# Start places of the normed rows, rows of a norm by transposes, and the order of the last sums, in a two-layer hybrid trunk on one core

## The chip, the core and the metric

The kernel runs on one core of one Trainium2 chip. TensorE (PE in the profile; PEld is its weight load) multiplies, VectorE (DVE), ScalarE (ACT) and GpSimd (POOL) do the elementwise work, SyncE (SP) issues most DMAs. The metric is the device time of one execution in microseconds, lower is better. All arrays are float32; the large products are made from two roundings of each operand (below).

## What is computed

A trunk of two layers on 512 tokens of width 1024. Layer 0 mixes tokens with a gated delta rule, layer 1 with sliding-window attention on a key and value projected once from layer 0's result; each layer ends with a gated MLP with a short causal convolution.

```python
def rmsnorm(x, w):
    xf = x.astype(jnp.float32)
    y = xf * lax.rsqrt(jnp.mean(xf * xf, axis=-1, keepdims=True) + EPS)
    return (y * w.astype(jnp.float32)).astype(x.dtype)

def conv_gated_mlp(hn, w_up, conv_w, conv_b, w_down):
    u = causal_dwconv(hn @ w_up, conv_w, conv_b)
    gate, val = jnp.split(u, 2, axis=-1)
    return (jax.nn.silu(gate) * val) @ w_down

def reference(x, ...):
    h = x
    for layer in range(2):
        if layer == 0:
            h = h + gated_deltanet(rmsnorm(h, a_norm_w[0]), ...)
        else:
            k_sh, v_sh = shared_kv(h, kv_norm_w, w_kv)
            h = h + sliding_window_sink_attention(rmsnorm(h, b_norm_w[0]), k_sh, v_sh, ...)
        h = h + conv_gated_mlp(rmsnorm(h, ffn_norm_w[layer]), ...)
    return rmsnorm(h, final_norm_w)
```

## The kernel before

The residual `h` lies transposed: eight tiles of 128 features by 512 tokens. A norm is split: `normed` (L888) multiplies each tile by the norm's weight and splits it into a rounded part (`xh`, ScalarE, L175) and the remainder (`xl`, VectorE, L176); the factor of each token, 1/rms, is applied after the product. So a normed input is sixteen rows of 128 x 512, eight `xh` and eight `xl`. The helper `row(tag)` (L110) takes each from a ring of eight buffers, and every buffer is exactly 2048 bytes per partition.

A product with a normed input is `mm3` (L161): for each of the eight k, three matmuls with 512 columns,

```python
PE.matmul(ps, hi[:, k, :m], xh[k], start=first and k == 0, stop=False)
PE.matmul(ps, hi[:, k, :m], xl[k][:], start=False, stop=False)
done.append(PE.matmul(ps, lo[:, k, :m], xh[k], start=False, stop=last and k == kt - 1))
```

which are L165, L166 and L167 of the profile; `hi` and `lo` (`whi`, `wlo`) are the weights, split in the same way by `cast` (L131, lines L135 on ScalarE and L136 on VectorE). The stationary operand is the weight block, the moving one is the row of the normed input. `mm3` serves the projections of the delta rule (until about 460 us), the up-projections of both MLPs (about 520 to 820 us and 1040 to 1330 us) and the key and value projection; the queries of attention have the same three matmuls in `one_by_one` (L1307, L1309, L1311). The down-projections (L1051 to L1053) have 256 columns and rows from other tags.

The factor of a norm comes in two functions. `rstd_cols` (L856) sums squares over the eight tiles, turns the sum into one column per block of 128 tokens (four matmuls with one column, L867), and gives `rt`, 128 x 4, by a square root and a reciprocal. `rstd_rows` (L873) spreads `rt` over all partitions: VectorE makes four scaled identities (L876, 128 x 512), TensorE multiplies a block of ones with them (L883, plain float32, 512 columns, two instructions), and ScalarE copies the result to `rstd` (L885, tile `p6s`). It is called three times: in both MLPs and in attention.

`final` (L1200) is the last norm. All but the last of the eight tiles have their weighted copy (`hw`) and their squares ready before the last down-projection, which is cut into two halves of 256 tokens (`last_down`, L960 to L962, twice for each half). When a half is done, `finish(u)` (L1230) weighs and squares the last tile's 256 tokens, turns the back four tiles of each block (L1218), sums the squares into columns (L1239), makes the factor (L1240 on ScalarE, L1241 on VectorE) and scales the turned blocks, the back half row on ScalarE (L1246), the front half row on VectorE (L1248); each half row goes out by its own DMA of 256 KB on SP (L1249).

The framework's scheduler orders each engine's instructions by priority, within the order of the code; `tc.high_priority` moves an instruction up, and `together` (L185) keeps a group in one piece on its engine; `behind(later, earlier)` (L179) fixes that one comes after another on the same engine without a semaphore.

Of the kernel before, what the change touches and what calls it, by code (L numbers as in the profile page):

```python
# [11 lines left out]
AF = mybir.ActivationFunctionType  # L12
ALU = mybir.AluOpType
# [4 lines left out]
P = 128  # L18
T = 512
NC = T // P  # L20
D = 1024
KD = D // P
EPS = 1e-6
# [21 lines left out]
def kernel(  # L45
# [27 lines left out]
    V, S, G, PE, SP = nc.vector, nc.scalar, nc.gpsimd, nc.tensor, nc.sync  # L73
# [9 lines left out]
    def nm(s):  # L83
        cnt[0] += 1
        return f"{s}_{cnt[0]}"
# [4 lines left out]
    main = ctx.enter_context(tc.tile_pool(name="main", bufs=1))  # L90
    PAIRS = {"sy": 4, "nt": 2, "kT": 2, "qT": 2, "at": 2, "ktok": 2, "vt": 2, "pz": 2, "m32": 1}
    ROWS = {
        "xh": 8,
        "xl": 8,
        "acc": 2,
        "sz": 2,
        "va": 2,
        "dt": 4,
        "ol": 1,
        "zl": 1,  # L100
# [6 lines left out]
        "f": 3,  # L107
    }

    def row(tag, dt=F32, n=T):  # L110
        return main.tile([P, n], dt, tag=tag, bufs=ROWS[tag], name=nm(tag))

    def pair(tag, dt=F32):
# [2 lines left out]
    def bank(tag):  # L116
        return psum.tile([P, T], F32, tag=tag, bufs=BANKS[tag], name=nm(tag))

    def const(shape, dt=F32, s="c"):
        return cp.tile(list(shape), dt, name=nm(s))  # L120
# [19 lines left out]
    def load_rows(w, tags):  # L140
        rows = [row(t)[:].rearrange("p (k c) -> p k c", k=2) for t in tags]
        for i, r in enumerate(rows):
            SP.dma_start(r, tiles_of(w, 2 * i * P, 2, 0))
        return rows
# [34 lines left out]
    def behind(later, earlier):  # L179
        info = mybir.DependencyInfo(mybir.DependencyClass.NoSync, mybir.DependencyReason.DATA)  # L180
        tc.add_manual_dep(later.ins, earlier.ins.name, info, reason="order of issue")
# [3 lines left out]
    def together(makes, *after):  # L185
        first = None
        for make in makes:
            if first is None:
                first = make()
                for a in after:  # L190
                    behind(first, a)
            else:
                with tc.high_priority(JUMP):
                    behind(make(), first)
# [16 lines left out]
    for i in range(2):  # L211
        cs = slice(HQK * P + i * P, HQK * P + (i + 1) * P)
# [4 lines left out]
    ident = const([P, P], s="ident")  # L217
# [3 lines left out]
    ones = const([P, P], s="ones")  # L221
    V.memset(ones[:], 1.0)
    epsc = const([P, 1], s="eps")
    V.memset(epsc[:], EPS)
    onec = ones[:, 0:1]
# [4 lines left out]
    def columns(parts, n, s, q=SP, tag="acc", place="g"):  # L230
        st = row(tag, n=P)
        r = 0
        for ap in parts:
            k = ap.shape[0]
            q.dma_start(st[r : r + k, :], ap)
            r += k
        ps = bank(place)
        PE.transpose(ps[:, :n], st[:n, :], ident[:n, :n])
        t = const([P, n], s=s)
        V.tensor_copy(t[:], ps[:, :n])  # L240
        return t
# [11 lines left out]
        q=S,  # L253
# [125 lines left out]
    def hc(ap):  # L379
# [397 lines left out]
    for pos, word in enumerate(" ".join(ORDER).split(), 1):  # L777
        name, _, later = word.partition("@")
        a, n = name[0], [int(d) for d in name[1:]]
# [33 lines left out]
    def nxt(role, tags):  # L813
        turn[role] = turn.get(role, -1) + 1
        return tags[turn[role] % len(tags)]

    def r2(role, dt=F32):
        return row(nxt(role, ROLES[role]), dt)
# [4 lines left out]
    def third_stage():  # L823
        return main.tile([P, 6, 256], F32, tag="st3", bufs=1, name=nm("st3"))
# [25 lines left out]
    for m in range(KD):  # L850
        x3 = xrows[m].rearrange("p (c e) -> p c e", c=NC)
        SP.dma_start(x3, x[0, :, m * P : (m + 1) * P].rearrange("(c p) e -> p c e", p=P))
        pt = bank("g")
        turn_row(pt, xrows[m])
        S.copy(hT[m], pt[:])
    def rstd_cols(h):  # L856
        acc = None
        for k in range(KD):
            sq = r2("sum" if acc is None else "hsq")
            S.activation(sq[:], h[k], AF.Square)  # L860
            if acc is None:
                acc = sq
            else:
                V.tensor_tensor(acc[:], acc[:], sq[:], op=ALU.add)
        ps = bank("g")
        for c in range(NC):
            PE.matmul(ps[:, c : c + 1], acc[:, c * P : (c + 1) * P], onec, start=True, stop=True)  # L867
        rt = const([P, NC], s="rt")
        S.activation(rt[:], ps[:, 0:NC], AF.Sqrt, bias=epsc[:, 0:1], scale=1.0 / D)
        V.reciprocal(rt[:], rt[:])  # L870
        return rt

    def rstd_rows(h):  # L873
        rt = rstd_cols(h)
        dg = third_stage()[:, 0:2, :].rearrange("p k c -> p (k c)")
        V.tensor_tensor(  # L876
            dg[:].rearrange("p (c t) -> p c t", c=NC),
            ident[:].unsqueeze(1).to_broadcast([P, NC, P]),
            rt[:].unsqueeze(2).to_broadcast([P, NC, P]),
            op=ALU.mult,  # L880
        )
        ps = bank("g")
        PE.matmul(ps[:], ones[:], dg[:], start=True, stop=True)  # L883
        r = r2("rstd")
        S.copy(r[:], ps[:])  # L885
        return r
# [291 lines left out]
    for m2 in range(KD // 2):  # L1178
        srcs = [tiles_of(a_w_out[0], 1024 * u, 8, 256 * m2) for u in range(2)]
        sts = [load_stage(a_w_out[0], 1024 * u, 8, 256 * m2) for u in range(2)]  # L1180
        if m2 < 2:
            for j in range(2):
                m = 2 * m2 + j
                ps = bank("d")
# [15 lines left out]
    def final(h, last_down):  # L1200
        hw, acc = [], None
        for k in range(KD):
            t = r2("xh")
            hw.append(t)
            if k == KD - 1:
                break
            V.tensor_scalar(t[:], h[k], onw_c[:, 9 + k : 10 + k], None, op0=ALU.mult)
            sq = r2("sum" if acc is None else "hsq")
            S.activation(sq[:], h[k], AF.Square)
            if acc is None:  # L1210
                acc = sq
            else:
                V.tensor_tensor(acc[:], acc[:], sq[:], op=ALU.add)

        def turned(hf, c, tag):
            pt = bank(tag)
            for k in range(4):
                PE.transpose(pt[:, k * P : (k + 1) * P], hw[4 * hf + k][:, c * P : (c + 1) * P], ident[:])  # L1218
            return pt

        CUTS = [(0, 2), (2, 4)]
        parts = [bank("d") for _ in CUTS]
        S.activation(warm[:], acc[:, 0:1], AF.Sqrt)
        front = [turned(0, c, t) for c, t in enumerate(["s", "s", "p", "g"])]
        h7, w7 = h[KD - 1], hw[KD - 1]
        sq7 = r2("hsq")
        rt = const([P, NC], s="rt")
        ts = [slice(a * P, b * P) for a, b in CUTS]

        def finish(u):  # L1230
            c0, c1 = CUTS[u]
            cs = slice(c0, c1)
            V.tensor_scalar(w7[:, ts[u]], h7[:, ts[u]], onw_c[:, 16:17], None, op0=ALU.mult)
            S.activation(sq7[:, ts[u]], h7[:, ts[u]], AF.Square)
            back = [turned(1, c, "s" if u and c % 2 else "d") for c in range(c0, c1)]
            ps = bank("g")
            for c in range(c0, c1):
                for x in (acc, sq7):
                    PE.matmul(ps[:, c : c + 1], x[:, c * P : (c + 1) * P], onec, start=x is acc, stop=x is sq7)  # L1239
            S.activation(rt[:, cs], ps[:, cs], AF.Sqrt, bias=epsc[:, 0:1], scale=1.0 / D)  # L1240
            V.reciprocal(rt[:, cs], rt[:, cs])  # L1241
            for c in range(c0, c1):
                for hf, pt in enumerate((front[c], back[c - c0])):
                    y = r2("xl")
                    if hf:
                        S.activation(y[:], pt[:], AF.Copy, scale=rt[:, c : c + 1])  # L1246
                    else:
                        V.tensor_scalar(y[:], pt[:], rt[:, c : c + 1], None, op0=ALU.mult)  # L1248
                    SP.dma_start(out[0, c * P : (c + 1) * P, hf * T : (hf + 1) * T], y[:])  # L1249

        n = len(CUTS)
        for u in range(n):
            ps = parts[u][:, 0 : ts[u].stop - ts[u].start]
            last_down(ps, ts[u], 0)
            if u > 0:
                finish(u - 1)
            last_down(ps, ts[u], 1)
            V.tensor_tensor(h7[:, ts[u]], h7[:, ts[u]], ps, op=ALU.add)
        finish(n - 1)


    Vp = main.tile([P, NC, 256], F32, tag="m32", bufs=1, name="Vp")
# [281 lines left out]
```

## Time and profile before

| | |
|---|---|
| median of the runs | 1399.07 us (1398.06 to 1400.09, 2 runs) |
| the profiled execution | 1399.55 us |
| its span on the core | 1397.4 us |
| granted TensorE clock over the span | 0.998 |
| VectorE, ScalarE, GpSimd busy | 82%, 55%, 1% of the span |

A matmul's busy time in the profile is longer than the step from one matmul to the next, since matmuls are pipelined. So for a dense stretch the reader takes the starts of consecutive matmuls in the timeline and subtracts them. A weight load runs beside the matmul ahead of it.

### The profile page before, as it was taken

The numbers are of one execution on the slowest core, as the hardware profiler recorded it, in microseconds if no ns is written. First come the engines' busy times: TensorE is split into PE (matmuls) and PEld (weight loads), VectorE is DVE, ScalarE is ACT, GpSimd is POOL, SyncE is SP. The second block draws the span as 40 slices with busy tenths as digits, with TensorE's granted clock in tenths as the row PEclk, the third lists the DMA queues.
The fourth block names the chain that finished last, engine by engine and source line by source line (L and its number), as shares of the span: only waits on it lengthen the run. The fifth ranks groups of instructions, "written<-read, shape, count | busy, mean of one in ns | idle before, by whom it ended". The sixth has DMA issues, their size and how long they took to land.

```text
span 1397.4 us, 22194 instructions
## 1 busy us (share of the span) xinstructions
PE 1374.6 (98%) x8514; PEld 1171.0 (84%) x8514; DVE 1144.3 (82%) x2153; ACT 765.6 (55%) x1482; POOL 15.2 (1%) x33
## 2 busy tenths in 40 slices
PE   7999999999999999999999999999999999999998
PEld 5788887888887898888988889877788889988897
DVE  4896896978967998879968899788668889878996
ACT  7766465757557455444344445677545444444543
POOL 1000000000100000000000000000000000000000
PEclk9999999999999999999999999999999999999999
DMA  5234154162567334221343223312132221432222
GB/s 162 83 114 134 50 173 141 64 197 91 171 192 225 127 119 140 94 88 52 130 151 121 76 84 114 121 62 69 61 113 91 91 95 63 146 106 80 96 76 76
DMA packets 164029, 154.97 MB, mean 111 GB/s; under 512 B 24340, under 2 KB 150869, under 8 KB 163925
## 3 DMA queue, kind: packets, MB, share of 16 engines
q1 hardware_dynamic: 161666, 153.37, 34.3%
q8 instruction: 67, 1.10, 0.3%
q10 hardware_dynamic: 2259, 0.20, 0.1%
q14 instruction: 37, 0.30, 0.1%
HBM read 136.74 MB, written 15.75 MB: 109 GB/s over the span
## 4 chain that ended last, share of the span: by engine, by line
PE 90%; DVE 4%; ACT 3%; DMA 2%; issue 1%; SPq 0%; DVEq 0%; ACTq 0%
PE d L165 19%; PE d L167 19%; PE d L166 19%; PE g L201 2%; PE d L1053 2%; PE d L1051 2%; PE d L1052 2%; PE s L1053 1%; PE s L1051 1%; PE s L1052 1%; PE d L1307 1%; PE d L1311 1%; PE d L1309 1%; PE g L1053 1%; PE g L1052 1%; PE g L1051 1%
## 5 line engine op out<-in xcount | busy, mean ns | idle before, releaser
L166 PE MATMUL d<-xl,whi 128*128 128x512 f32 x1128 | 443.0, 395 | 0.0
L165 PE MATMUL d<-xh,whi 128*128 128x512 f32 x1128 | 442.6, 395 | 0.4 <-DVE va L1284 0.3
L167 PE MATMUL d<-xh,wlo 128*128 128x512 f32 x1128 | 442.5, 394 | 0.0
L135 ACT CAST whi<-stage 128x1024 fp32r<-128x1024 f32 (+2 forms) x238 | 231.6, 977 | 224.9 <-PE d L166 129.3
L136 DVE TENSOR_TENSOR wlo<-stage,whi 128x1024 fp32r<-128x1024 f32 (+2 forms) x238 | 268.1, 1129 | 51.8 <-ACT whi L135 50.5
L165 PEld LDWEIGHTS d<-xh,whi 128*128 128x128 f32 x1128 | 211.7, 188 | 44.8 <-DVE va L1284 0.7
L167 PEld LDWEIGHTS d<-xh,wlo 128*128 128x128 f32 x1128 | 211.7, 188 | 44.5 <-DVE wlo L136 0.7
L166 PEld LDWEIGHTS d<-xl,whi 128*128 128x128 f32 x1128 | 211.7, 188 | 43.4 <-issue 0.7
L283 DVE SCALAR_TENSOR_TENSOR acc<-d,cwc,acc 128x511 f32<-128x511 f32 (+2 forms) x96 | 70.2, 738 | 5.2 <-ACT acc L280 4.5
L933 ACT ACTIVATE dt<-dt 128x512 f32<-128x512 f32 x44 | 27.8, 632 | 80.2 <-DVE dt L916 80.2
L911 DVE TENSOR_TENSOR sz<-d,p6s 128x512 f32<-128x512 f32 x58 | 39.9, 688 | 37.6 <-PE d L167 35.3
L916 DVE SCALAR_TENSOR_TENSOR va<-sz,fcw,va 128x511 f32<-128x511 f32 (+1 forms) x58 | 43.4, 747 | 1.7 <-ACT va L914 0.9
L916 DVE SCALAR_TENSOR_TENSOR dt<-sz,fcw,dt 128x511 f32<-128x511 f32 (+1 forms) x58 | 43.3, 746 | 1.7 <-ACT dt L914 0.9
L564 DVE TENSOR_TENSOR sT<-sT,p6s 64x31 f32<-64x31 f32 (+15 forms) x124 | 40.8, 329 | 1.6
L1376 ACT ACTIVATE dt<-dt,sm 128x256 f32<-128x256 f32 (+1 forms) x64 | 30.1, 471 | 21.5 <-DVE sm L1359 21.5
L558 DVE TENSOR_TENSOR p6s<-sN,sT 64x31 f32<-64x31 f32 (+15 forms) x124 | 40.6, 327 | 1.5
L135 ACT CAST whi<-st 128x768 fp32r<-128x768 f32 (+1 forms) x30 | 23.8, 792 | 31.5 <-PE g L1052 8.6
L911 DVE TENSOR_TENSOR zl<-d,p6s 128x512 f32<-128x512 f32 x30 | 20.6, 688 | 23.0 <-PE d L167 22.7
L693 ACT ACTIVATE rq<-o 128x128 f32<-128x128 f32 x64 | 19.0, 297 | 35.7 <-DVE o L688 26.1
L935 DVE TENSOR_TENSOR va<-dt,va 128x512 f32<-128x512 f32 x44 | 30.4, 690 | 1.3
L136 DVE TENSOR_TENSOR wlo<-st,whi 128x768 fp32r<-128x768 f32 (+1 forms) x30 | 26.9, 900 | 2.1 <-ACT whi L135 1.7
L914 ACT ACTIVATE dt<-sz,normc,fcw 128x512 f32<-128x512 f32 x29 | 23.6, 815 | 7.3 <-DVE sz L911 7.1
(859 smaller groups left out, 2975.6 us busy)
## 6 DMA issues: line engine op xcount, KB each, us to landing
stage<-in_ffn_w_up_dram SPq DMA_DIRECT2D x44, 1024.0 KB, 5.0
stage<-in_a_w_in_dram SPq DMA_DIRECT2D x23, 1024.0 KB, 5.2
stage<-in_ffn_w_down_dram SPq DMA_DIRECT2D x16, 768.0 KB, 4.9
stage<-in_a_w_out_dram SPq DMA_DIRECT2D x8, 1024.0 KB, 6.0
st<-in_ffn_w_down_dram SPq DMA_DIRECT2D x8, 768.0 KB, 5.2
zd<-sz SPq DMA_DIRECT2D x16, 256.0 KB, 2.0
od<-o SPq DMA_DIRECT2D x16, 256.0 KB, 2.4
stage<-in_b_w_q_dram SPq DMA_DIRECT2D x4, 1024.0 KB
```

The lines of the kernel that those rows point to most:

```text
L135: S.copy(hi[:, :kt, :m], src)
L136: V.tensor_tensor(lo[:, :kt, :m], src, hi[:, :kt, :m].bitcast(F32), op=ALU.subtract)
L165: PE.matmul(ps, hi[:, k, :m], xh[k], start=first and k == 0, stop=False)
L166: PE.matmul(ps, hi[:, k, :m], xl[k][:], start=False, stop=False)
L167: done.append(PE.matmul(ps, lo[:, k, :m], xh[k], start=False, stop=last and k == kt - 1))
L283: V.scalar_tensor_tensor(acc[:, d:], ps[:, : T - d], col, acc[:, d:], op0=ALU.mult, op1=ALU.add)
L564: V.tensor_tensor(Tm[:, s + 1 : 32, 0:m], Tm[:, s + 1 : 32, 0:m], tv, op=ALU.subtract)
L911: V.tensor_tensor(u[:], ps[:], rs[:], op=ALU.mult)
L916: V.scalar_tensor_tensor(acc[:, d:], u[:, : T - d], tap(2 - d, t), acc[:, d:], op0=ALU.mult, op1=ALU.add)
L1051: PE.matmul(ps, w[0][:, wk, :], hi, start=first and k == 0, stop=False, **kw)
L1052: PE.matmul(ps, w[0][:, wk, :], lo, start=False, stop=False, **kw)
L1053: PE.matmul(ps, w[1][:, wk, :], hi, start=False, stop=k == n - 1, **kw)
```

## The change

It has three parts.

**Places.** A buffer of `xh` or `xl` gets 16 elements more (2112 bytes, 64 more than a multiple of 512), and the row is a view that begins 0 to 12 elements into it. In the built program of before, the sixteen rows begin at 0 modulo 512 bytes, and so do all other tiles of the pool and the weight tiles `whi` and `wlo`. After, the rows begin at

| row k | 0 | 1 | 2 | 3 | 4 | 5 | 6 | 7 |
|---|---|---|---|---|---|---|---|---|
| `xh`, bytes modulo 512 | 0 | 64 | 128 | 192 | 256 | 336 | 416 | 496 |
| `xl`, bytes modulo 512 | 8 | 80 | 160 | 240 | 288 | 320 | 384 | 448 |

and all other tiles of the pool still at 0 modulo 512. Of each pair, one begins at a multiple of 64 bytes and the other 8, 16, 32 or 48 bytes off one.

**Rows of the norm.** `rstd_rows` makes its rows by four transposes of a column of `rt` that is repeated 128 times, in place of the scaled identities and the product with ones.

**The end.** In `finish`, the sums of squares move ahead of the last tile's transposes; for the second half, the sum over seven tiles and that over the last one go to banks of their own and the first enters the square root as its bias, column by column; the front half row of block 1 moves from the first to the second half, behind the last tile's weighing; the last half row's DMA goes out on ScalarE's queue.

```diff
+    SHIFTS = {"xh": [0, 0, 0, 0, 0, 4, 8, 12], "xl": [2, 4, 8, 12, 8, 0, 0, 0]}
+    taken = {"xh": 0, "xl": 0}
+
     def row(tag, dt=F32, n=T):
+        if tag in SHIFTS:
+            t = main.tile([P, T + 16], dt, tag=tag, bufs=ROWS[tag], name=nm(tag))
+            d = SHIFTS[tag][taken[tag] % 8]
+            taken[tag] += 1
+            return t[:, d : d + n]
         return main.tile([P, n], dt, tag=tag, bufs=ROWS[tag], name=nm(tag))
...
     def rstd_rows(h):
         rt = rstd_cols(h)
-        dg = third_stage()[:, 0:2, :].rearrange("p k c -> p (k c)")
-        V.tensor_tensor(
-            dg[:].rearrange("p (c t) -> p c t", c=NC),
-            ident[:].unsqueeze(1).to_broadcast([P, NC, P]),
-            rt[:].unsqueeze(2).to_broadcast([P, NC, P]),
-            op=ALU.mult,
+        ps = bank("g")
+        together(
+            [
+                lambda c=c: PE.transpose(ps[:, c * P : (c + 1) * P], rt[:, c : c + 1].to_broadcast([P, P]), ident[:])
+                for c in range(NC)
+            ]
         )
-        ps = bank("g")
-        PE.matmul(ps[:], ones[:], dg[:], start=True, stop=True)
         r = r2("rstd")
         S.copy(r[:], ps[:])
         return r
...
-        def finish(u):
-            c0, c1 = CUTS[u]
-            cs = slice(c0, c1)
-            V.tensor_scalar(w7[:, ts[u]], h7[:, ts[u]], onw_c[:, 16:17], None, op0=ALU.mult)
+        def finish(u, left):
+            cs, at = range(*CUTS[u]), slice(*CUTS[u])
             S.activation(sq7[:, ts[u]], h7[:, ts[u]], AF.Square)
-            back = [turned(1, c, "s" if u and c % 2 else "d") for c in range(c0, c1)]
-            ps = bank("g")
-            for c in range(c0, c1):
-                for x in (acc, sq7):
-                    PE.matmul(ps[:, c : c + 1], x[:, c * P : (c + 1) * P], onec, start=x is acc, stop=x is sq7)
-            S.activation(rt[:, cs], ps[:, cs], AF.Sqrt, bias=epsc[:, 0:1], scale=1.0 / D)
-            V.reciprocal(rt[:, cs], rt[:, cs])
...
+            weighed = V.tensor_scalar(w7[:, ts[u]], h7[:, ts[u]], onw_c[:, 16:17], None, op0=ALU.mult)
+            if left:
+                behind(left(), weighed)
+            back = {c: bank("s" if u and c % 2 else "d") for c in cs}
+            for c in cs:
+                turn_into(back[c], 1, c, range(3))
+            ps = bank("d" if u else "g")
+            if u:
+                sums = bank("g")
+                columns_of(sums, acc, cs)
+                V.tensor_scalar(rest[:, at], sums[:, at], 1.0 / D, EPS, op0=ALU.mult, op1=ALU.add)
+                summed = columns_of(ps, sq7, cs)
...
+            for c in cs:
+                behind(turn_into(back[c], 1, c, [3]), summed[-1])
+            if u:
+                for c in cs:
+                    S.activation(rt[:, c : c + 1], ps[:, c : c + 1], AF.Sqrt, bias=rest[:, c : c + 1], scale=1.0 / D)
+                    V.reciprocal(rt[:, c : c + 1], rt[:, c : c + 1])
+            else:
+                S.activation(rt[:, at], ps[:, at], AF.Sqrt, bias=epsc[:, 0:1], scale=1.0 / D)
+                V.reciprocal(rt[:, at], rt[:, at])
...
+                q = S if hf and c == NC - 1 else SP
+                q.dma_start(out[0, c * P : (c + 1) * P, hf * T : (hf + 1) * T], y[:])
...
+            for c in cs:
+                half_row(c, 1, back[c])
+                if u or c == 0:
+                    half_row(c, 0, front[c])
+            return lambda: half_row(1, 0, front[1])
```

The places move no instruction. The other two parts do, at two places. In the first MLP's first up-projections, TensorE's rows before the change (`g` is the bank that becomes the norm's rows, `d` the bank of an up-projection, `st` the scaled identities):

```order
L165 MATMUL d_5520<-xh_5419,whi_5516 128x512
L166 MATMUL d_5520<-xl_5420,whi_5516 128x512
L167 MATMUL d_5520<-xh_5419,wlo_5517 128x512
L165 MATMUL d_5520<-xh_5423,whi_5516 128x512
L883 MATMUL g_5472<-st_880_5470,ones_88 128x512
L166 MATMUL d_5520<-xl_5424,whi_5516 128x512
```

and after it:

```order
L173 MATMUL d_5521<-xh_5419,whi_5517 128x512
L886 MATMUL g_5470<-ident_81,rt_5467 128x128 x4
L174 MATMUL d_5521<-xl_5420,whi_5517 128x512
L175 MATMUL d_5521<-xh_5419,wlo_5518 128x512
L173 MATMUL d_5521<-xh_5423,whi_5517 128x512
L174 MATMUL d_5521<-xl_5424,whi_5517 128x512
```

The four transposes stand where the product with ones stood, three matmuls earlier; VectorE's L876 ahead of them is gone.

At the end of the program, VectorE's rows before (`pz` holds the last tile of `h`, the tiles `xl` are half rows of the output):

```order
L1241 RECIPROCAL rt_13584<-rt_13584 128x2
L1248 TENSOR_SCALAR xl_13653<-s_13563,rt_13584 128x512
L1248 TENSOR_SCALAR xl_13659<-s_13568,rt_13584 128x512
L1258 TENSOR_TENSOR pz_4516<-pz_4516,d_13561 128x256
L1233 TENSOR_SCALAR xh_13559<-pz_4516,onwc_367 128x256
L1241 RECIPROCAL rt_13584<-rt_13584 128x2
L1248 TENSOR_SCALAR xl_13697<-p_13573,rt_13584 128x512
L1248 TENSOR_SCALAR xl_13703<-g_13578,rt_13584 128x512
```

and after:

```order
L1270 RECIPROCAL rt_13587<-rt_13587 128x2
L1277 TENSOR_SCALAR xl_13659<-s_13566,rt_13587 128x512
L1295 TENSOR_TENSOR pz_4516<-pz_4516,d_13564 128x256
L1245 TENSOR_SCALAR xh_13562<-pz_4516,onwc_367 128x256
L1277 TENSOR_SCALAR xl_13680<-s_13567,rt_13587 128x512
L1255 TENSOR_SCALAR rt_13587<-g_13692 128x2
L1267 RECIPROCAL rt_13587<-rt_13587 128x1 x2
L1277 TENSOR_SCALAR xl_13707<-p_13568,rt_13587 128x512
L1277 TENSOR_SCALAR xl_13713<-g_13569,rt_13587 128x512
```

One half row moves from ahead of the last addition to behind the last weighing, and the sum's part over seven tiles (L1255) is a new step of VectorE ahead of the reciprocals.

More of the change, by code (lines that the diff above doesn't have):

```diff
@@ L1213, in final, with turn_into, columns_of @@
                 V.tensor_tensor(acc[:], acc[:], sq[:], op=ALU.add)
[L1215 to L1219, printed above, removed]
+        def turn_into(pt, hf, c, ks):
+            for k in ks:
+                last = PE.transpose(pt[:, k * P : (k + 1) * P], hw[4 * hf + k][:, c * P : (c + 1) * P], ident[:])
+            return last
+        def columns_of(ps, x, cs):
+            one = lambda c: PE.matmul(ps[:, c : c + 1], x[:, c * P : (c + 1) * P], onec, start=True, stop=True)
+            return [one(c) for c in cs]
         CUTS = [(0, 2), (2, 4)]
@@ L1223, in final @@
         S.activation(warm[:], acc[:, 0:1], AF.Sqrt)
-        front = [turned(0, c, t) for c, t in enumerate(["s", "s", "p", "g"])]
+        front = [bank(t) for t in ("s", "s", "p", "g")]
+        for c, pt in enumerate(front):
+            turn_into(pt, 0, c, range(4))
         h7, w7 = h[KD - 1], hw[KD - 1]
         sq7 = r2("hsq")
-        rt = const([P, NC], s="rt")
+        both = const([P, 2 * NC], s="rt")
+        rt, rest = both[:, 0:NC], both[:, NC : 2 * NC]
         ts = [slice(a * P, b * P) for a, b in CUTS]
-        def finish(u):
-            c0, c1 = CUTS[u]
-            cs = slice(c0, c1)
-            V.tensor_scalar(w7[:, ts[u]], h7[:, ts[u]], onw_c[:, 16:17], None, op0=ALU.mult)
+        def finish(u, left):
+            cs, at = range(*CUTS[u]), slice(*CUTS[u])
@@ L1242, in finish @@
[L1242 to L1249, printed above, removed]
+            weighed = V.tensor_scalar(w7[:, ts[u]], h7[:, ts[u]], onw_c[:, 16:17], None, op0=ALU.mult)
@@ new lines, in finish @@
+            if left:
[11 more added lines that the diff above has]
+                for c in cs:
+                    for x in (acc, sq7):
+                        one = x[:, c * P : (c + 1) * P]
+                        summed = [PE.matmul(ps[:, c : c + 1], one, onec, start=x is acc, stop=x is sq7)]
@@ new lines, in finish, with half_row @@
+            for c in cs:
[4 more added lines that the diff above has]
+                    V.reciprocal(rt[:, c : c + 1], rt[:, c : c + 1])
+            else:
+                S.activation(rt[:, at], ps[:, at], AF.Sqrt, bias=epsc[:, 0:1], scale=1.0 / D)
+                V.reciprocal(rt[:, at], rt[:, at])
+            def half_row(c, hf, pt):
+                y = r2("xl")
+                if hf:
+                    scaled = S.activation(y[:], pt[:], AF.Copy, scale=rt[:, c : c + 1])
+                else:
+                    scaled = V.tensor_scalar(y[:], pt[:], rt[:, c : c + 1], None, op0=ALU.mult)
+                q = S if hf and c == NC - 1 else SP
+                q.dma_start(out[0, c * P : (c + 1) * P, hf * T : (hf + 1) * T], y[:])
+                return scaled
@@ L1251, in final @@
+            for c in cs:
+                half_row(c, 1, back[c])
+                if u or c == 0:
+                    half_row(c, 0, front[c])
+            return lambda: half_row(1, 0, front[1])
         n = len(CUTS)
@@ L1255, in final @@
             if u > 0:
-                finish(u - 1)
+                left = finish(u - 1, None)
             last_down(ps, ts[u], 1)
             V.tensor_tensor(h7[:, ts[u]], h7[:, ts[u]], ps, op=ALU.add)
-        finish(n - 1)
+        finish(n - 1, left)
     Vp = main.tile([P, NC, 256], F32, tag="m32", bufs=1, name="Vp")
```

## The prediction

> **What bounds the kernel now.** I read the page's first part, then the chain of work that ended last, then the groups, and last the timeline of single matmuls.
>
> ```profile
> PE 1374.6 (98%) x8514; PEld 1171.0 (84%) x8514; DVE 1144.3 (82%) x2153; ACT 765.6 (55%) x1482; POOL 15.2 (1%) x33
> ...
> PE 90%; DVE 4%; ACT 3%; DMA 2%; issue 1%; SPq 0%; DVEq 0%; ACTq 0%
> PE d L165 19%; PE d L167 19%; PE d L166 19%; PE g L201 2%; PE d L1053 2%; PE d L1051 2%; PE d L1052 2%; PE s L1053 1%; PE s L1051 1%; PE s L1052 1%; PE d L1307 1%; PE d L1311 1%; PE d L1309 1%; PE g L1053 1%; PE g L1052 1%; PE g L1051 1%
> ...
> L166 PE MATMUL d<-xl,whi 128*128 128x512 f32 x1128 | 443.0, 395 | 0.0
> L165 PE MATMUL d<-xh,whi 128*128 128x512 f32 x1128 | 442.6, 395 | 0.4 <-DVE va L1284 0.3
> ```
>
> TensorE carries 90% of the chain, and L165 to L167, the matmuls on the normed rows, carry 57% alone. They wait for nothing (0.0 and 0.4 us idle before 1128 of them). So the time changes if the step from one matmul to the next changes, if TensorE gets other work, or if the tail behind the last matmul changes. Here is the step in a dense stretch of the first MLP:
>
> ```profile
> 600.06 0.39 PE L165 MATMUL d<-xh,whi 128*128 128x512 f32 x1
> 600.29 0.39 PE L166 MATMUL d<-xl,whi 128*128 128x512 f32 x1
> 600.51 0.39 PE L167 MATMUL d<-xh,wlo 128*128 128x512 f32 x1
> 600.74 0.39 PE L165 MATMUL d<-xh,whi 128*128 128x512 f32 x1
> ```
>
> Three steps in 0.68 us, 227 ns each. In the same stretch VectorE and ScalarE are busy most of the time, and the step does not move: it is not set by what they do. The change touches 1128 x 3 matmuls of L165 to L167 and the queries' L1307, L1309 and L1311, 64 each (row below): 3576 in all. One nanosecond on each is 3.6 us.
>
> **Part 1, the places.** No instruction is added or moved, so all of it is the price of a matmul (or of a write) whose row begins elsewhere. In before every one of these rows begins at the same place modulo 512 bytes, so the trace cannot show the new ones directly. The nearest rows are these: a matmul of the delta rule, L468, whose moving operand `mnegr` begins 160 bytes off a multiple of 512 (32 off a multiple of 64), and a plain float32 product, L646, which passes 256 columns twice.
>
> ```profile
> L166 PE MATMUL d<-xl,whi x1128: 387/389/798, 15.1 to 1331.7; 128*128 128x512 f32 x187, 128*48 128x512 f32 x1
> ...
> L468 PE MATMUL g<-mnegr,identr x16: 388/394/400, 52.5 to 319.9; 128*128 128x512 f32 x16
> ...
> L646 PE MATMUL s<-S,kT x48: 377/379/484, 152.2 to 422.3; 128*128 128x256 f32 x48
> ...
> L1307 PE MATMUL d<-xh,whi x64: 389/393/501, 895.2 to 970.9; 128*128 128x512 f32 x64
> ```
>
> Minimum, median and maximum: the row off its place has 388 to 400 ns with a median of 394, against 389 on place, while L646 has 379 for as many columns passed. The timeline around one L468, in a stretch that steps at 227 before it:
>
> ```profile
> 106.64 0.39 PE L166 MATMUL d<-xl,whi 128*128 128x512 f32 x1
> 106.87 0.39 PE L467 MATMUL g<-gr,skr 128*128 128x512 f32 x1
> 107.10 0.40 PE L468 MATMUL g<-mnegr,identr 128*128 128x512 f32 x1
> 107.33 0.39 PE L165 MATMUL d<-xh,whi 128*128 128x512 f32 x1
> 107.56 0.40 PE L166 MATMUL d<-xl,whi 128*128 128x512 f32 x1
> 107.80 0.39 PE L167 MATMUL d<-xh,wlo 128*128 128x512 f32 x1
> 108.03 0.39 PE L165 MATMUL d<-xh,whi 128*128 128x512 f32 x1
> 108.25 0.39 PE L166 MATMUL d<-xl,whi 128*128 128x512 f32 x1
> ```
>
> From 106.87 to 108.03 stand five steps in 1.16 us, 232 ns each, then 227 again. So the step is not a constant of the instruction: a pair with other places costs some 5 ns a step until the stream is regular again. The steps go further down and up than that: 0.22 us in the first pair of rows here, and 0.706 us for three in the run whose weights have 48 columns, all its rows on place.
>
> ```profile
> 208.40 0.39 PE L165 MATMUL d<-xh,whi 128*128 128x512 f32 x1
> 208.62 0.39 PE L166 MATMUL d<-xl,whi 128*128 128x512 f32 x1
> ...
> 22.21 0.40 PE L165 MATMUL d<-xh,whi 128*48 128x512 f32 x1
> 22.44 0.40 PE L166 MATMUL d<-xl,whi 128*48 128x512 f32 x1
> 22.68 0.40 PE L167 MATMUL d<-xh,wlo 128*48 128x512 f32 x1
> 22.91 0.40 PE L165 MATMUL d<-xh,whi 128*48 128x512 f32 x1
> ```
>
> Bounds of the price: below, 10 ns less on each matmul (389 to 379, as if the step could fall to L646's), 3576 x 10 = 36 us less; above, the 48-column run's 235 against 227 on each, 3576 x 8.5 = 30 us more. I take zero: the median instance of L468 off place is within its own scatter of the matmuls that are on place beside it (0.39 and 0.40 both occur in both), it never falls below 388, and the step in the dense stretch is so regular that I see no conflict for a new place to remove. [...]
>
> Writes of the rows on ScalarE and VectorE and reads of output rows by the DMA get the same new places. They cost nothing here as long as TensorE is what ends last: VectorE is idle for 18% of the span, some 250 us, and it writes such a row only 40 times.
>
> **Part 2, the norm's rows.** Removed, three times: a VectorE step (L876), which lies beside TensorE's matmuls, and a product with ones in two instructions (L883). Added: four transposes. The cost on TensorE is the time from the first of them to the matmul after next, less that one's 0.23 us:
>
> ```profile
> 525.43 1.02 PE L883 MATMUL g<-st,ones 128*128 128x512 f32 x2
> 525.89 0.80 PE L166 MATMUL d<-xl,whi 128*128 128x512 f32 x1
> 526.52 0.40 PE L167 MATMUL d<-xh,wlo 128*128 128x512 f32 x1
> ...
> 215.95 0.60 PE L201 MATMUL g<-ident,ol 128*128 128x128 f32 x4
> 216.31 0.47 PE L167 MATMUL d<-xh,wlo 128*128 128x512 f32 x1
> 216.62 0.39 PE L165 MATMUL d<-xh,whi 128*128 128x512 f32 x1
> ```
>
> L883: 526.52 - 525.43 - 0.23 = 0.86 us. Four transposes between such matmuls (L201): 216.62 - 215.95 - 0.23 = 0.44 us. Gain 0.42 us, three times 1.3 us, all on the path, since TensorE is dense at these places. The rows of the norm also come earlier; nothing on TensorE waits for them, so that earns nothing. The bound on the other side is no gain, if the repeated column is slow to load as weights. [...]
>
> **Part 3, the end.** The rows of the tail, from VectorE's two half rows to the last square root and the DMAs:
>
> ```profile
> 1387.99 1.41 DVE L1248 TENSOR_SCALAR xl<-s,rt 128x512 f32<-128x512 f32 x2
> 1388.70 5.52 SPq L1249 DMA_DIRECT2D out_dram<-xl  x8
> 1388.71 0.28 PE L962 MATMUL d<-S,wlo 128*128 128x256 f32 x1
> 1389.31 0.41 DVE L1258 TENSOR_TENSOR pz<-pz,d 128x256 f32<-128x256 f32 x1
> 1389.76 0.42 ACT L1234 ACTIVATE acc<-pz 128x256 f32<-128x256 f32 x1 [0.50 <-DVE pz L1258]
> 1391.21 0.26 ACT L1240 ACTIVATE rt<-g,eps 128x2 f32<-128x2 f32 x1 [1.03 <-PE g L1239]
> ```
>
> The last matmul ends at 1388.99, but the addition L1258 starts at 1389.31, behind the second half row of VectorE (0.7 us). That half row moves behind the weighing: the addition starts some 0.3 us earlier. The new step on VectorE (the sum of seven tiles) then stands behind the moved half row: 1389.03 + 0.41 + 0.35 + 0.7 + a small one of about 0.2 gives 1390.7 with gaps, so the square root starts at about 1390.8 instead of 1391.21: 0.4 us. TensorE's two sums of the last tile are done by then. The roots and reciprocals, now column by column, cost one step more (0.26) ahead of the second block, but the first block's half rows don't wait for it. Of the DMAs, the moved one goes earlier than the last four as before, and the very last no longer stands in SP's queue (eight issues in 5.52 us, 0.7 each) but on ScalarE's, which has nothing behind it. I count 0.4 us; bounds 0 (the second column waits for the moved half row's engine) and 1.1 (0.4 and an issue of 0.7).
>
> **The sum.** 0 - 1.3 - 0.4 = -1.7 us against the profiled execution's 1399.55 us (span 1397.4): 1397.8 us. That execution is 0.5 us above the median of 1399.07, less than the runs differ, so I forecast 1397.8.
>
> **Rivals.**
> - The regular step is lost (slower than before). The 227 ns hold where all rows share one place; in after each pair has one row off a multiple of 64 bytes: `xl` of five pairs (one matmul in three) and `xh` of three (two in three), 11 matmuls of 24, or 1639. At L468's 394 against 389, 5 ns each, that is 8.2 us: 1406.0. If each also disturbs those behind it, as after 107.10 (five steps of 232), all 3576 pay 5 ns: 18 us and 1415.7. It decides as soon as the mean extra exceeds 0.5 ns (1.7 us). For it: 106.87 to 108.03. Against it: single instances of L468 at 388.
> - The step falls a little: 0.22 us instead of 0.227 occurs in before, where a matmul comes after an irregular one. If different places let matmuls start without a common rhythm, I take 2.5 ns on each (the 0.22 is rounded), 9 us: 1389. For it: 208.40 to 208.62. Against it: such steps are rare and follow longer ones.
> [...]
> - All matmuls step as the 48-column run: 30 us, 1428. Against it: those rows were on place, so their cause is another one.
>
> **How the numbers follow.** My forecast (places cost nothing) 0.34; the regular step lost 0.30; the small fall 0.23; the large fall 0.08; the 48-column step 0.05. The range leaves out the last two (0.13) and the upper end of the lost step and the lower of the small fall (some 0.06): 1387 to 1414. The forecast's own range is 1396 to 1400. What a measurement tells from no change here is about 2%, 28 us: faster by that only in the large fall (0.08), slower in the last case (0.05), within it 0.87.
>
> **What would show it.** Places: in the dense stretches of the MLPs the starts of three consecutive matmuls, 0.68 us apart in all (forecast), 0.70 or more (lost), 0.675 or less (small fall), 0.65 (large). L166's median duration beside 389 says the same for all. Norm's rows: from the first transpose to the second matmul behind it 0.67 us instead of 1.09. End: the addition starts right at the last matmul's end, and the last square roots about 2.1 us after the last matmul's start instead of 2.5. I am wrong if the median of L165 to L167 moves by 3 ns or more, whichever way.

## The result, and the profile after

| | before | after |
|---|---|---|
| time, median of 2 runs | 1399.07 us (1398.06 to 1400.09) | 1410.72 us (1410.12 to 1411.33) |
| ratio, with its 95% interval | 1 | 1.0089 (1.0072 to 1.0107) |
| span of the profiled execution | 1397.4 us | 1407.9 us |
| median of L165, now L173 | 389 ns | 394 ns |

The changed kernel is 11.7 us slower. The forecast was 1397.8 us; what came is the rival called "the regular step is lost", inside the range and less than the 2% that the chances speak of.

First the page of the kernel after: the busy times of the engines, the chain of work that ended last, and the three costliest groups (busy time, mean of one, idle time before).

```profile
PE 1385.0 (98%) x8520; PEld 1169.3 (83%) x8520; DVE 1143.9 (81%) x2152; ACT 764.8 (54%) x1483; POOL 15.1 (1%) x33
...
PE 92%; DVE 2%; DMA 2%; ACT 2%; issue 1%; DVEq 0%; SPq 0%; ACTq 0%
...
L173 PE MATMUL d<-xh,whi 128*128 128x512 f32 x1128 | 447.0, 399 | 0.2 <-ACT xh L183 0.2
L174 PE MATMUL d<-xl,whi 128*128 128x512 f32 x1128 | 446.3, 398 | 0.0
L175 PE MATMUL d<-xh,wlo 128*128 128x512 f32 x1128 | 446.0, 397 | 0.0
```

TensorE is busy 10.4 us longer (1374.6 before), VectorE and ScalarE are as busy as before, and the three groups still wait for next to nothing (0.2 us in all): no new wait, but dearer matmuls. L173 to L175 are L165 to L167 of before; their means rise from 395, 395 and 394 to 399, 398 and 397. The view by line of the kernel after (minimum, median, maximum in ns) shows which matmuls became dearer:

```profile
L174 PE MATMUL d<-xl,whi x1128: 387/394/585, 15.3 to 1342.4; 128*128 128x512 f32 x187, 128*48 128x512 f32 x1
L174 PE MATMUL d<-sy,whi x36: 389/389/397, 430.1 to 1033.7; 128*128 128x512 f32 x36
```

The rows `xl`, whose places changed, have a median of 394 instead of 389; the row `sy`, which the same line passes against the same weights and whose place did not change, still has 389. The steps in a dense stretch of the kernel after:

```profile
740.12 0.40 PE L173 MATMUL d<-xh,whi 128*128 128x512 f32 x1
740.36 0.39 PE L174 MATMUL d<-xl,whi 128*128 128x512 f32 x1
740.59 0.39 PE L175 MATMUL d<-xh,wlo 128*128 128x512 f32 x1
740.83 0.39 PE L173 MATMUL d<-xh,whi 128*128 128x512 f32 x1
```

Three steps take 0.71 us where they took 0.68. How much that is on average is read from a long stretch. The last MLP has 480 such matmuls with nothing between them; here are its first and last row, before:

```profile
1223.33 0.40 PE L165 MATMUL d<-xh,whi 128*128 128x512 f32 x1
...
1331.93 0.39 PE L167 MATMUL d<-xh,wlo 128*128 128x512 f32 x1
```

and after:

```profile
1231.41 0.39 PE L173 MATMUL d<-xh,whi 128*128 128x512 f32 x1
...
1342.64 0.39 PE L175 MATMUL d<-xh,wlo 128*128 128x512 f32 x1
```

479 steps take 108.60 us before and 111.23 after: 226.7 ns and 232.2 ns each, 5.5 ns more. This "dense step" (first to last start of these 480, by 479) is the measure that the experiments below use, since it needs no comparison of whole runs.

The other two parts did what they should. The norm's rows after, on TensorE:

```profile
525.06 0.60 PE L886 MATMUL g<-ident,rt 128*128 128x128 f32 x4
525.41 0.47 PE L174 MATMUL d<-xl,whi 128*128 128x512 f32 x1
525.72 0.39 PE L175 MATMUL d<-xh,wlo 128*128 128x512 f32 x1
```

From the first transpose to the second matmul behind it 0.66 us (0.67 predicted, 1.09 before). And the end after, in the timeline of all engines:

```profile
1399.74 0.28 PE L968 MATMUL d<-S,wlo 128*128 128x256 f32 x1
...
1400.06 0.42 DVE L1295 TENSOR_TENSOR pz<-pz,d 128x256 f32<-128x256 f32 x1 [0.46 <-PE d L968]
...
1400.79 0.75 DVE L1277 TENSOR_SCALAR xl<-s,rt 128x512 f32<-128x512 f32 x1
...
1401.45 0.15 DVE L1255 TENSOR_SCALAR rt<-g 128x2 f32<-128x2 f32 x1
...
1401.69 0.41 ACT L1266 ACTIVATE rt<-d,rt 128x1 f32<-128x1 f32 x2 [0.76 <-DVE rt L1255]
```

The addition L1295 now waits for the last matmul itself and starts 0.04 us behind its end (1399.74 + 0.28). The roots start 1.95 us after the last matmul's start (2.5 before, 2.1 predicted). From that matmul's start to the end of the span it is 8.21 us (1399.74 to 1407.95), where it was 8.68 (1388.71 to 1397.39): 0.47 us gained.

### The profile page after: what moved, and what is told of

Same layout as the page of the kernel before. It is cut to its first block, busy times and chain, and to the rows that moved or that the text cites. A ratio compares the mean times of both kernels' runs of the same rounds, so it can differ in the third digit from the quotient of the medians.

```text
span 1407.9 us, 22206 instructions
## 1 busy us (share of the span) xinstructions
PE 1385.0 (98%) x8520; PEld 1169.3 (83%) x8520; DVE 1143.9 (81%) x2152; ACT 764.8 (54%) x1483; POOL 15.1 (1%) x33
## 4 chain that ended last, share of the span: by engine, by line
PE 92%; DVE 2%; DMA 2%; ACT 2%; issue 1%; DVEq 0%; SPq 0%; ACTq 0%
PE d L173 20%; PE d L174 20%; PE d L175 20%; PE d L1059 2%; PE d L1057 2%; PE d L1058 2%; PE g L209 2%; PE s L1059 2%; PE s L1057 2%; PE s L1058 2%; PE d L1344 1%; PE d L1348 1%; PE d L1346 1%; PE g L1058 1%; PE g L1059 1%; PE g L1057 1%
## 5 line engine op out<-in xcount | busy, mean ns | idle before, releaser
L173 PE MATMUL d<-xh,whi 128*128 128x512 f32 x1128 | 447.0, 399 | 0.2 <-ACT xh L183 0.2
L175 PE MATMUL d<-xh,wlo 128*128 128x512 f32 x1128 | 446.0, 397 | 0.0
L173 PEld LDWEIGHTS d<-xh,whi 128*128 128x128 f32 x1128 | 211.8, 188 | 49.6 <-issue 0.6
L175 PEld LDWEIGHTS d<-xh,wlo 128*128 128x128 f32 x1128 | 211.5, 188 | 48.8 <-DVE wlo L144 0.7
```

## The experiments

Three theories stood for the 5 ns: the dense step depends on the place of a row itself, off a multiple of 512 or of 64 (E, for each row); on the places changing from one row to the next (C); or on the distance between the row that passes and the weight block, modulo some number of bytes (D). The first expectations call them A or A1, A2, and B; the "one more fetch" that two of them name as a cause is a guess, no run shows it. In all kernels from here on to the two single parts, parts 2 and 3 stay as in the kernel after; only places differ. The dense step of each, and the time (the first four have 10, 4, 4 and 4 runs, the others one):

| kernel | rows `xh`, `xl` modulo 512 | weights modulo 512 | dense step, ns | time, us |
|---|---|---|---|---|
| no places | 0 | 0 | 226.7 | 1394.32 |
| pitch only | the eight multiples of 64, one for each row of a tag | 0 | 231.2 | 1407.31 |
| all at 32 | 32 | 0 | 233.3 | 1412.30 |
| `xl` at 32 | 0, 32 | 0 | 231.1 | 1406.78 |
| all at 64 | 64 | 0 | 233.3 | 1406.08 |
| all at 128 | 128 | 0 | 232.4 | 1410.27 |
| weights at 32 | 0 | 32 | 233.3 | 1412.81 |
| both at 32 | 32 | 32 | 226.7 | 1395.07 |
| all at 256 | 256 | 0 | 226.7 | 1394.30 |
| all at 448 | 448 | 0 | 233.4 | 1416.31 |
| next fits | 0, 32 | `whi` 0, `wlo` 32 | 232.3 | 1408.99 |
| own fits | 0, 32 | `whi` 32, `wlo` 0 | 233.3 | 1411.71 |

The dense step is that of one stretch. The MLPs have four more stretches of 250 to 550 such matmuls, and in most kernels they step alike within 0.1 ns. The exceptions are `xl` at 32, which has 231.7 and 233.3 ns in two of them, all at 128, which has 233.4 in one, and all at 64, which has 228.9 in three.

The kernel before had 1396.7 us beside the first eight of these (13 runs), 1397.4 beside the two at 256 and 448 and the two single parts (23 runs), and 1396.3 beside the last two (one run).

**No places.** The kernel after, with the rows' code of before:

```diff
-        if tag in SHIFTS:
-            t = main.tile([P, T + 16], dt, tag=tag, bufs=ROWS[tag], name=nm(tag))
...
-            return t[:, d : d + n]
         return main.tile([P, n], dt, tag=tag, bufs=ROWS[tag], name=nm(tag))
```

> The changed kernel with all sixteen rows back at 0 modulo 512 bytes (2048 bytes each); the norm's rows by transposes and the end's new order stay. Theory (the places alone made it slower, by lengthening the step of the matmuls on the rows): the dense step in the MLPs is 227 ns again, and the time is 1.7 us under before, about 1397.5 us. Rival (a part of the loss comes from the other two parts): over 1400 us, with the step at 227 ns.

The ratio to before is 0.9978 (0.9968 to 0.9988): faster than both kernels, by 3.1 us and about 15.5 us (1.0089 by 0.9978 is 1.0111). Its dense stretch, first and last row:

```profile
1217.34 0.40 PE L165 MATMUL d<-xh,whi 128*128 128x512 f32 x1
...
1325.94 0.39 PE L167 MATMUL d<-xh,wlo 128*128 128x512 f32 x1
```

108.60 us for the 479 steps, as before the change. So the places are the whole loss. (The span of this profile, 1391.0 us, is 6.4 us under that of before, more than the medians differ: before was granted a clock of 0.97 between 42 and 100 us, this one 1.00.)

Against the kernel after, by the two spans it is 16.9 us: the norm's rows of the first MLP start at 520.59 here and at 525.06 after, 4.5 us apart, over some 1210 matmuls of these lines (0.8 us of it is a later first matmul, 9.77 against 8.98 us); the other 12.4 us lie behind, 11.5 of them in the five dense stretches of the MLPs, which take 464.65 us here and 476.12 after with 2053 matmuls in each (5.6 ns a step).

**Pitch only.** The buffers keep their 2112 bytes, the rows begin at their start:

```diff
-    SHIFTS = {"xh": [0, 0, 0, 0, 0, 4, 8, 12], "xl": [2, 4, 8, 12, 8, 0, 0, 0]}
+    SHIFTS = {"xh": [0] * 8, "xl": [0] * 8}
```

> The changed kernel with all shifts 0 and the buffers still 2112 bytes: the rows begin at the eight multiples of 64 modulo 512, xh and xl of a pair at the same one. Theory A (a row's place modulo 64 bytes counts): step 227 ns, time as without places, about 1397.5 us. Theory B (the place modulo 512 counts, against the weights, which all begin at 0): the step stays at 231 to 233 ns and the time at about 1410 us. Anything between: both count.

```profile
1230.27 0.39 PE L173 MATMUL d<-xh,whi 128*128 128x512 f32 x1
...
1341.00 0.39 PE L175 MATMUL d<-xh,wlo 128*128 128x512 f32 x1
```

Ratio 1.0077 (1.0061 to 1.0092), 110.73 us for the 479 steps: rows that all begin at multiples of 64 bytes cost nearly as much as those of the change. "Off a multiple of 64", on which the prediction's rival counted, is not the condition.

**All at 32.** Eight floats ahead of the sixteen rows, 120 behind them, all at one place again:

```diff
-        h, l = row("xh", F32R), row("xl", F32R)
+        if k == 0:
+            main.tile([P, 8], F32, tag="pad_a", bufs=1, name="pad_a")
+        h = row("xh", F32R)
+        l = row("xl", F32R)
+        if k == 0:
+            main.tile([P, 120], F32, tag="pad_c", bufs=1, name="pad_c")
```

> As without places, but all sixteen rows begin at 32 modulo 512 bytes. Theory A1 (the place modulo 64 counts by itself, a row off a multiple of 64 needs one more fetch): step well over 227 ns, 230 to 234, time 1408 us or more. Theory A2 (only differences between rows that follow each other count): step 227 ns, about 1397.5 us.

```profile
1231.74 0.40 PE L165 MATMUL d<-xh,whi 128*128 128x512 f32 x1
...
1343.51 0.39 PE L167 MATMUL d<-xh,wlo 128*128 128x512 f32 x1
```

Ratio 1.0118 (1.01 to 1.0136), and 233.3 ns a step with rows that all share one place: no change between rows is needed for the loss.

**`xl` at 32.** The eight floats stand between `xh` and `xl`, so `xh` stays at 0:

```diff
-        h, l = row("xh", F32R), row("xl", F32R)
+        h = row("xh", F32R)
+        if k == 0:
+            main.tile([P, 8], F32, tag="pad_b", bufs=1, name="pad_b")
+        l = row("xl", F32R)
+        if k == 0:
+            main.tile([P, 120], F32, tag="pad_c", bufs=1, name="pad_c")
```

> As without places, but the eight xl rows begin at 32 modulo 512 bytes and the eight xh rows at 0. Theory A1 (each row off a multiple of 64 costs): a third of the matmuls are off, step about 229 to 230 ns on average, 1404 to 1407 us. Theory A2 (differences count): two of three transitions change, step 230 ns or more, time over 1407 us, over that of all rows at 32.

Ratio 1.0078 (1.0063 to 1.0093), dense step 231.1 ns, 4.4 more than at 0. Neither expectation came out: the step is above the 229 to 230 of A1, and the time is not above that of all rows at 32, as A2 had it. In this stretch one row in three off costs two thirds of what three in three cost (6.6 ns), and in the third of the five stretches, with 233.3 ns, all of it: the loss isn't paid by the displaced matmul alone.

**All at 64, all at 128.** As "all at 32", with 16 and 32 floats ahead and 112 and 96 behind.

> As without places, but all sixteen rows begin at 64 modulo 512 bytes; read from the dense step of the MLPs. With a buffer pitch of 2112 and no shifts the step was 231. Theory C (a change of place from one row to the next costs): 227 ns here, since nothing changes. Theory D (the distance of a row from the weights' place, modulo 256 or 512, costs): a constant step over 227, some 228 to 233 ns, and a time about 1400 to 1410 us.

> As without places, but all sixteen rows begin at 128 modulo 512 bytes. Theory C: step 227 ns. Theory D: a constant step, over 227, other than at 64 if the distance modulo 256 sets it.

One place for all, a multiple of 64 or 128, and the loss is there: 233.3 and 232.4 ns. That rules out theory C, and with it a condition on multiples of 64.

**Weights at 32, and both at 32.** The first leaves the rows at 0 and moves the weight tiles by a shorter gap; the second has that gap and the rows of "all at 32":

```diff
-    wpool.tile([P, 120], F32, tag="gap", bufs=1, name="gap_w")
+    wpool.tile([P, 112], F32, tag="gap", bufs=1, name="gap_w")
```

> Rows at 0, but the weight tiles (and the tiles that they are loaded into) begin at 32 modulo 512 bytes. Theory D (the distance between row and weights counts): step 233 ns as with the rows at 32, and more time in the down-projections too. Theory E (a row's own place counts: off a multiple of 64 it takes one more fetch): step 227 ns, time as without places, or a little over if weights off a multiple of 64 load more slowly.

> Rows and weight tiles both at 32 modulo 512 bytes. Theory D: step 227 ns, since the distance is 0 again. Theory E: step 233 ns as with the rows alone at 32.

The stretch with the weights at 32:

```profile
1233.13 0.40 PE L165 MATMUL d<-xh,whi 128*128 128x512 f32 x1
...
1344.89 0.40 PE L167 MATMUL d<-xh,wlo 128*128 128x512 f32 x1
```

and with rows and weights at 32:

```profile
1218.57 0.39 PE L165 MATMUL d<-xh,whi 128*128 128x512 f32 x1
...
1327.16 0.39 PE L167 MATMUL d<-xh,wlo 128*128 128x512 f32 x1
```

This pair decides between the theories. With the rows at the places of before and only the weights moved, the step is 233.3 ns; with both moved by the same 32 bytes it is 226.7 again. In these kernels a row's own place doesn't decide the step; its distance to the weights does. (One part of the expectation did not come: with the weights at 32 the down-projections did not take more time but less, as the last section shows.)

**All at 256, all at 448.** As "all at 32", with 64 and 112 floats ahead and 64 and 16 behind.

> Rows all at one place, 256 bytes off a multiple of 512, weights at 0; parts 2 and 3 in. If the distance between the moving row and the weights counts modulo 256, the step of the dense stretches is 227 ns and the time that of the kernel without the places, 1394 to 1395 us. If it counts modulo 512, the step is 229 to 233 ns and the time 1404 to 1412 us.

> Rows all 64 bytes ahead of a multiple of 512 (448), weights at 0; parts 2 and 3 in. If the distance counts whichever its sign, the step is 229 to 233 ns as with the rows 64 behind, and the time 1404 to 1412 us. If a row ahead of the weights is cheaper than one behind, the step falls to 227 ns or under it, and the time to 1395 us or less.

The stretch with the rows at 256:

```profile
1218.27 0.40 PE L165 MATMUL d<-xh,whi 128*128 128x512 f32 x1
...
1326.87 0.39 PE L167 MATMUL d<-xh,wlo 128*128 128x512 f32 x1
```

and at 448:

```profile
1237.22 0.40 PE L165 MATMUL d<-xh,whi 128*128 128x512 f32 x1
...
1349.00 0.39 PE L167 MATMUL d<-xh,wlo 128*128 128x512 f32 x1
```

A distance of 256 is as good as 0 (226.7 ns at both), as it must be if the distance counts modulo 256 bytes; no second pair of distances 256 apart was run. A row 64 bytes ahead of the weights is no cheaper than one 64 behind: it has 233.3 ns in all five stretches, the other in two of them. (The single time, 1416.31 us, lies above the 1404 to 1412 that was expected, and the step at the upper end of 229 to 233.) No distance that was tried steps shorter than 226.7 ns.

**Next fits, own fits.** Which block is it: the one that the row is multiplied with, or the next matmul's, which is loaded beside it (in the kernel before, L166's weight load and L165's matmul both start at 600.06 us)? Pads between `whi` and `wlo` set the two kinds apart, with `xl` at 32. In "next fits":

```diff
         hi = wpool.tile([P, 8, P], F32R, tag="whi", bufs=3, name=nm("whi"))
+        if "pad_w" not in passed:
+            passed.add("pad_w")
+            wpool.tile([P, 8], F32, tag="pad_w", bufs=1, name="pad_w")
         lo = wpool.tile([P, 8, P], F32R, tag="wlo", bufs=3, name=nm("wlo"))
```

with the gap of 112; in "own fits" eight floats stand ahead of `whi` and 120 between the two.

> Parts 2 and 3 in; xh and whi at 0, xl and wlo at 32 modulo 512. The matmuls go xh with whi, xl with whi, xh with wlo; the weights loaded beside them are the next one's: whi, wlo, whi. If the next matmul's weights count, every distance is 0: step 226.7 ns and 1394 to 1396 us. If the row's own weights count, two of three are 32 off: step 231 to 233 ns, 1404 us or more.

> Parts 2 and 3 in; xh and wlo at 0, xl and whi at 32 modulo 512. To the row's own weights two of three matmuls have distance 0, as in the kernel with xl alone at 32 (step 231.3 ns there); to the next matmul's weights none has. If the row's own weights count, the step is about 231 ns and the time about 1407 us. If the next matmul's count, all three are 32 off: step 233.3 ns, 1409 to 1413 us.

```profile
1229.91 0.40 PE L170 MATMUL d<-xh,whi 128*128 128x512 f32 x1
...
1341.16 0.39 PE L172 MATMUL d<-xh,wlo 128*128 128x512 f32 x1
```

and in "own fits":

```profile
1232.74 0.40 PE L172 MATMUL d<-xh,whi 128*128 128x512 f32 x1
...
1344.49 0.40 PE L174 MATMUL d<-xh,wlo 128*128 128x512 f32 x1
```

With every next block at distance 0 the step is 232.3 ns ("next fits"), so the next block is not all that counts. In "own fits" it is 233.3 in all five stretches, not the 231 that was expected if the own block alone counts. But `xl` at 32, which also has one matmul in three at distance 32 to its own block, had 233.3 itself in one stretch of five, so this does not rule out that the own block alone counts. A distance to either block may be enough; the runs don't separate the two, and that stays open.

**Norm's rows alone, end alone.** The kernel before with one part each: `rstd_rows` as after, or `finish` as after.

```diff
-        dg = third_stage()[:, 0:2, :].rearrange("p k c -> p (k c)")
...
+        ps = bank("g")
+        together(
+            [
+                lambda c=c: PE.transpose(ps[:, c * P : (c + 1) * P], rt[:, c : c + 1].to_broadcast([P, P]), ident[:])
+                for c in range(NC)
+            ]
         )
-        ps = bank("g")
-        PE.matmul(ps[:], ones[:], dg[:], start=True, stop=True)
```

> The kernel before with the norm's rows alone made by four transposes; places of the rows and the end as before. The prediction's sum: three times 0.42 us less, 1.3 us, a ratio of 0.9991 (1.0 if the transposes gain nothing, 0.9978 if all that the kernel with parts 2 and 3 gained comes from here). The step of the dense stretches stays at 227 ns.

> The kernel before with the new order of the end alone; places of the rows and the norm's rows as before. The prediction's sum: 0.4 us less; from the traces of the kernels with the new end, 0.53 to 0.57 us from the last matmul's start to the end of the span: a ratio of 0.9996. If this and the norm's rows together give less than 2 us, some of the 3 us of the kernel with both is a shift of the stages ahead of the first MLP and belongs to neither.

The norm's rows alone, on TensorE:

```profile
524.39 0.60 PE L878 MATMUL g<-ident,rt 128*128 128x128 f32 x4
524.75 0.48 PE L166 MATMUL d<-xl,whi 128*128 128x512 f32 x1
525.06 0.39 PE L167 MATMUL d<-xh,wlo 128*128 128x512 f32 x1
```

0.67 us, that is 0.44 without the matmul's own 0.23, as predicted. At the two other calls the kernel after has as much: 0.68 (892.53 to 893.21) and 0.67 (1042.23 to 1042.90). The end alone:

```profile
1386.64 0.28 PE L962 MATMUL d<-S,wlo 128*128 128x256 f32 x1
...
1386.96 0.42 DVE L1289 TENSOR_TENSOR pz<-pz,d 128x256 f32<-128x256 f32 x1 [0.45 <-PE d L962]
...
1388.60 0.41 ACT L1260 ACTIVATE rt<-d,rt 128x1 f32<-128x1 f32 x2 [0.76 <-DVE rt L1249]
```

The roots start 1.96 us after the last matmul's start, and from there to the end of the span (1394.78) it is 8.14 us, 0.54 less than before. The ratios are 0.9992 (0.998 to 1.0005) and 0.9996 (0.9986 to 1.0007): 1.1 and 0.6 us less, which whole runs can't tell from nothing, but the rows above can. Their sum, 1.7 us, is the predicted one, and lies at the lower end of what the kernel without the places gained (0.9968 to 0.9988 is 1.7 to 4.5 us); whether its 3.1 us hold more than the two parts is not settled.

## Why the prediction was wrong

- **What bounds the kernel** was right: TensorE's step on L165 to L167, no wait. One nanosecond on each of 3576 matmuls was put at 3.6 us; the 15.5 us that the places cost are 4.3 ns on each.
- **Part 1, the step that failed.** "I take zero: the median instance of L468 off place is within its own scatter of the matmuls that are on place beside it", and "the step in the dense stretch is so regular that I see no conflict for a new place to remove". The nearest row had it right: 394 against 389 ns and steps of 232 ns were quoted, and the kernel after has 394 and 232.2. Two errors of reading led away from it. The rows "beside" L468 at 0.40 were themselves in the disturbed stretch (106.87 to 108.03), so they were no sample of matmuls on place. And a stretch without a visible conflict bounds only the gain: it says that nothing is left to remove, not that nothing can be added.
- **The rival "the regular step is lost"** named the effect and its size: 8.2 us if the displaced rows alone pay, 18 us and 1415.7 if all do. The second is the closer: 15.5 us. Its count of rows was wrong, since it took those off a multiple of 64; pitch only and all at 64 show that these multiples cost too (231.2 and 233.3 ns). Nor do the rows begin where the table ahead of the prediction has them: in the program built from the kernel after, the rows k = 0 to 7 of the MLPs begin at 384, 320, 256, 192, 128, 80, 32, 496 (`xh`) and 392, 336, 288, 240, 160, 64, 0, 448 (`xl`). By the distance modulo 256, 21 matmuls of 24 are displaced there, not 11. In L468 itself, `mnegr` (160) and its weights `identr` (288 modulo 512) are 128 bytes apart, a distance that all at 128 showed to cost (232.4 ns); that it was also off a multiple of 64 explains nothing here.
- **The gains that the prediction weighed** (2.5 ns, or 10 ns to L646's level) did not come in any of the tried distances: 226.7 ns was the shortest dense step, so no run shows the step of the large fall, 10 ns shorter, that the chances count with 0.08. That L646's 379 ns are "for as many columns passed" is not shown either: 379 is the median of one instruction, and the trace gives it 256 columns.
- **Writes and reads at the new places** cost nothing, as predicted: the split's ScalarE half of `xh` from `h` has a median of 716 ns before and after, VectorE's half of `xl` 744 and 747, VectorE's half row of the output (from bank `s`) 747 and 748, and the output's DMAs take 2.0 us from issue to landing in both.
- **Part 2** was right: 0.43 us for four transposes in place of 0.86 (0.44 predicted). A duration is not the cost here: each of these transposes lasts 272 ns (the median of L886), but the next starts 0.11 us behind it (four span 0.60 us), so the cost of four is not four durations.
- **Part 3** was right in its mechanism and a little short: 0.47 us in the kernel after and 0.54 with the end alone, where 0.4 was predicted. The sum's new step on VectorE (L1255) took 0.15 instead of the 0.2 put down, and the roots came 0.15 us earlier than the 2.1 us.
- **The sum** was -1.7 us for the last two parts; the single parts measured -1.1 and -0.6. What the sum lacked was only the places.

The trace before had a second row that pointed at the failed step, and the prediction did not read it. L467, just ahead of L468, passes `gr`, which begins at 0, against weights `skr` that begin at 96 to 156 modulo 512 in the built program. None of its 16 instances is under 392 ns:

```profile
L467 PE MATMUL g<-gr,skr x16: 392/395/501, 52.3 to 319.6; 128*128 128x512 f32 x16
```

It is no clean measure, since its weights are one column repeated and L468 follows it each time. But it is a row on its place that is as dear as the one off it, which is what a distance to the weights would give.

What the places do in the chip is not shown. Measured is the step alone: 226.7 ns where rows and weight blocks stand 0 or 256 bytes apart, and 228.9 to 233.4 ns in the kernels where some or all of them stand at another distance, for the same instructions.

## What to carry to other kernels

In a kernel that TensorE's dense stream of float32 rows with 512 columns bounds, try the start of the moving row 0 or 256 bytes from that of the weight block: here these two distances had 226.7 ns a step, and every other that was tried cost 2 to 7 ns more, about 1% of the kernel. Before a layout is changed, look for any pair of operands in the trace that already stands at another distance, the weights' place included, and take its difference as the price even where single rows scatter as much. A neat regular stretch bounds what a change can gain there, not what it can cost; and small edits sent together with a layout change are best read from their own rows, since whole runs did not resolve 0.5 or 1 us.

## What the runs showed that was not expected

The matmuls that pass only 256 columns, in the down-projections, prefer the other case. A stretch of 424 of them in the kernel without places, first and last row:

```profile
1166.40 0.28 PE L1049 MATMUL d<-at,whi 128*128 128x256 f32 x1
...
1217.21 0.28 PE L1051 MATMUL p<-m,wlo 128*128 128x256 f32 x1
```

and with the weights at 32, the rows at 0:

```profile
1182.85 0.28 PE L1049 MATMUL d<-at,whi 128*128 128x256 f32 x1
...
1233.01 0.28 PE L1051 MATMUL p<-m,wlo 128*128 128x256 f32 x1
```

423 steps take 50.81 and 50.16 us: 120.1 ns at distance 0 and 118.6 ns at 32. The other long stretches of down-projections in these two kernels differ the same way, by 1.5 to 1.7 ns. The kernel with both at 32 has this gain too (its `xh` and `xl` moved with the weights, the rows of the down-projections did not), and still is not faster than the one without places in its single run (1395.07 us). Some of the gain goes back where L166 passes 512 columns of rows that stayed at 0, as the view by line of that kernel shows:

```profile
L166 PE MATMUL d<-xl,whi x1128: 387/389/580, 15.0 to 1326.9; 128*128 128x512 f32 x187, 128*48 128x512 f32 x1
L166 PE MATMUL d<-sy,whi x36: 392/396/428, 426.6 to 1024.4; 128*128 128x512 f32 x36
```

The displaced `xl` have 389 there, and `sy`, which was not moved, 396: the reverse of the kernel after, which is the theory of the distance once more.

The rows at 64 have two steps within one run of the same kernel: 233.3 ns in the stretch of 480 matmuls that the table has and in one more, but 228.9 in the other three, of which this is the second (287 matmuls, 65.46 us):

```profile
583.44 0.39 PE L166 MATMUL d<-xl,whi 128*128 128x512 f32 x1
...
648.90 0.39 PE L167 MATMUL d<-xh,wlo 128*128 128x512 f32 x1
```

So a distance has no fixed price. That would explain why the single time of that kernel, 1406.08 us, lies under the 1412.30 of the rows at 32, which have 233.3 in all five stretches. What decides which step a stretch falls into, the runs don't show.
